# Two operand slices of block 2 spread over block 0's gate steps, the split of blocks 2 and 3's gate operands swapped between VectorE and GpSimd, and the last outputs stored as whole rows

## The chip, the cores and the metric

The kernel runs on one core of a Trainium2 chip. The metric is the time of one execution on the device, in microseconds (us). A profile comes from one further execution, recorded by the hardware; its times are counted from the start of its span.

## What is computed

One layer of a streaming encoder over 2048 prompt tokens and 32 sample tokens, 1024 wide. Cut to the parts that matter here (g_mlp and g_final are weights, p an extra input of 256 columns):

```python
h = x + merge(attention(rmsnorm(x, g_attn) @ w_in)) @ w_out
c = rmsnorm(h, g_mlp)
h = h + square(relu(c @ w_up)) @ w_down
h = h + sigmoid(h @ w_ple_gate) * (p @ w_ple_proj)      # the "gate"
y = rmsnorm(h, g_final)                                 # outputs y_prompt, y_sample
```

All tensors are float32. The keys and values of the attention are outputs too; they are not touched by the change.

## The kernel before, in words

The 2080 tokens are worked in four blocks (0 to 3; 512, 512, 512 and 544 tokens). Activations lie transposed, features on the partitions, in slices of 128 features (index k, 8 slices for 1024).

**Products.** Every float32 operand is split in a high part (ScalarE copies it to the matmul's type, L181) and a low part, raw minus high. The low part is made by GpSimd in pieces of at most 272 columns (`pool_tt`, L166 and L176) or by VectorE in one instruction (L187). Each product is three matmuls (`mm3`): high x high at L216, weight's high x activation's low at L217, weight's low x activation's high at L218. A weight unit is loaded raw into one of four buffers (`wr`) and split in two halves into `piece` tiles from a ring. All DMAs are issued by SyncE (SP), in its order.

**The gate** (`gate`, from L1327) of a block first splits the 8 slices of h into `hu` (block 0 has them made earlier; block 3 puts them in `hc`), then makes 8 steps d: a weight unit of `w_ple_gate`, 24 matmuls into `gps` (8 slices k x 3), the sigmoid of it by ScalarE (L1366 to L1371) and VectorE (L1370), 6 matmuls into `pps`, and VectorE's product (L1385), added to h by GpSimd. Step d's weights are split in two halves of four slices each: the first half serves k = 0 to 3, the second k = 4 to 7.

**What runs beside block 0's gate.** The MLP of block 2 (`mlp7`) works on seven sums and differences of the quarters of its operand c, held split in tiles `cs` for the whole MLP. `cparts` makes them slice by slice, four slices in all, two of which are made earlier. One slice is 2 loads `tmp<-hS` and 2 normalisations on VectorE (L1021), 4 sums (L1033 to L1036, VectorE), and 7 splits of 256 columns: high parts on ScalarE, 5 low parts on VectorE, 2 on GpSimd. The four sums form a chain, since each overwrites a quarter that the next reads. The first step of `mlp7` loads the first two w_up units and makes sums of them (L1259 to L1262, VectorE) and their splits (`lead`). `weave(main, side, 1)` takes one step of the side generator after each step of the main one; with `along` as the side, gate steps 1 and 2 are each followed by a slice of `cparts`, step 3 by nothing, step 4 by the first step of `mlp7` (the gate's step 0 is taken ahead of the weave).

**The order.** The program is written as such generators, and a scheduler then places each engine's instructions with a timeline of its own; so an engine's order is not the written one, and it is shown below where it matters. Each engine then works strictly in that order.

**The end.** `final` (L1393) of block 3 transposes h back, sums the squares, and scales: per 128 tokens the left 512 columns by ScalarE in place (`yn`, L1434), the right 512 by VectorE from the accumulator into `yo` (L1436), each then stored by a DMA of its own, 10 in all.

Of the kernel before, what the change touches and what calls it, by code (L numbers as in the profile page):

```python
# [13 lines left out]
F32 = mybir.dt.float32  # L14
# [6 lines left out]
P = 128  # L21
D = 1024
# [12 lines left out]
BLK = 544  # L35
# [64 lines left out]
def weave(main, side, step, i=0, n=1):  # L100
    for _ in main:
        if i % step == 0:
            for _ in range(n):
                next(side, None)
        i += 1
    drain(side)
# [37 lines left out]
class Kern:  # L144
# [1182 lines left out]
    def gate(self, b, h, up, act, md, wk=None, made=None):  # L1327
        nc, a = self.nc, self.a
        n, t0 = BN[b], 512 * b
# [5 lines left out]
        if made is not None:  # L1335
            hH, hL = made
        elif wk is None and act.aw is None:
            hc = [act.tile([P, 4, 272], F32R, tag="cs", name="hc").rearrange("p a b -> p (a b)") for _ in range(8)]
            hH, hL = [[hc[4 * i + k // 2][:, BLK * (k % 2) : BLK * (k % 2) + n] for k in range(8)] for i in range(2)]
        elif wk is None:  # L1340
            hH = act.tile([P, 8, act.aw], F32R, tag="act", name="hH")
            hL = act.tile([P, 8, act.aw], F32R, tag="act", name="hL")
            hH, hL = [[t[:, k, :n] for k in range(8)] for t in (hH, hL)]
        else:
            hH, hL = [[up.tile([P, BLK], F32R, tag="u", name="hu")[:, :n] for k in range(8)] for _ in range(2)]
        if made is None:
            for k in range(8):
                self.split(hH[k], hL[k], h[:, k, :n], "act", "dve" if k % 2 else "pool")
        for dq in range(2):
            ph, pl = self.wunit(  # L1350
                Wp[:, 512 * dq : 512 * dq + 512].rearrange("(k p) c -> p k c", p=P), [2, 512]
# [38 lines left out]
                        self.pool_tt(hv, hv, sg, ALU.add)  # L1390
                yield

    def final(self, b, h, up, fk, mm, md=None):  # L1393
        nc, a = self.nc, self.a
        t0 = 512 * b
        sts, yns = {}, {}
        phased = md is not None

        def side(c0, tn, q):
            if phased:  # L1400
                sts[c0] = st_all[:, c0 // P]
            elif q == 0:
                sts[c0] = fk.tile([P, 2], F32, tag="fst", bufs=6, name="fst")
            st = sts[c0]
            yp = (md if phased and q == 1 else mm).tile([P, 512], F32, tag="mm", name="yp")
            for k in range(4):
                nc.tensor.transpose(yp[:tn, P * k : P * k + P], h[:, 4 * q + k, c0 : c0 + tn], self.ident)  # L1407
            if phased and q == 1:
                yns[c0, q] = yp
            else:  # L1410
                yns[c0, q] = up.tile([P, BLK], F32, tag="u", name="yn")[:, :512]
                if phased:
                    nc.vector.tensor_tensor(yns[c0, q][:tn], yp[:tn], self.gf[:tn, :512], op=ALU.mult)
                else:
                    nc.vector.tensor_copy(yns[c0, q][:tn], yp[:tn])
            junk = up.tile([P, BLK], F32, tag="u", name="junk")[:tn, :512]
            nc.scalar.activation(junk, yp[:tn], AF.Square, accum_out=st[:tn, q : q + 1])

        if phased:
            st_all = fk.tile([P, 5, 2], F32, tag="fsa", name="fsa")  # L1420
            nc.gpsimd.memset(st_all, 1.0)
            for c0, tn in toks(b):
                side(c0, tn, 0)
                yield
        def emit(c0, tn, r):
            tt = t0 + c0
            dst = a["y_prompt"][0, tt : tt + tn] if tt < SP else a["y_sample"][0, tt - SP : tt - SP + tn]
            for q in range(2):
                src = yn = yns[c0, q]
                if phased and q == 1:  # L1430
                    yn = up.tile([P, BLK], F32, tag="u", name="yo")[:, :512]
                g = self.gf[:tn, 512 * q : 512 * q + 512]
                if phased and q == 0:
                    nc.scalar.activation(yn[:tn], src[:tn], AF.Copy, scale=r)  # L1434
                else:
                    nc.vector.scalar_tensor_tensor(yn[:tn], src[:tn], r, g, op0=ALU.mult, op1=ALU.mult)  # L1436
                self.dma(dst[:, 512 * q : 512 * q + 512], yn[:tn])

        if phased:
            for c0, tn in toks(b):  # L1440
                side(c0, tn, 1)
            ss = fk.tile([P, 5], F32, tag="fss", name="fss")
            nc.vector.tensor_tensor(ss, st_all[:, :, 0], st_all[:, :, 1], op=ALU.add)
            r = self.rsqrt(fk, ss, 5, 1.0 / D, EPS, nc.vector, "rfa")
            for i, (c0, tn) in enumerate(toks(b)):
                emit(c0, tn, r[:tn, i : i + 1])
            return
        for c0, tn in toks(b):
            side(c0, tn, 0)
            side(c0, tn, 1)  # L1450
            st = sts[c0]
            nc.vector.tensor_tensor(st[:tn, 0:1], st[:tn, 0:1], st[:tn, 1:2], op=ALU.add)
            emit(c0, tn, self.rsqrt(fk, st[:tn, 0:1], 1, 1.0 / D, EPS, nc.vector, "rf", tn, 5))
            yield

    def run(self):
        tc, nc, a = self.tc, self.nc, self.a
        with ExitStack() as top:
# [180 lines left out]
            next(g)  # L1639
            box = []  # L1640
            m = self.mlp7(2, hh[1], box, ops[2], wk, up, mm, md)
            weave(g, self.along(c, m), 1)
            f = self.final(0, h, up, fk, mm)
            for _ in range(2):
                next(m)
            h = box[0]
# [12 lines left out]
            h = box[0]  # L1659
            weave(m, f, 1)  # L1660
            g = self.gate(3, h, up, cs, md)
            f = self.final(3, h, up, fk, mm, md)
            for _ in range(5):
                next(g)
            for _ in range(3):
# [46 lines left out]
```

## Time and profile before

| what | value |
|---|---|
| time, median of 3 executions | 3150.33 us (3146.29 to 3152.24) |
| the profiled execution's own time | 3146.42 us |
| its span | 3144.6 us |
| TensorE busy | 3011.4 us, 96% of the span |
| VectorE, ScalarE, GpSimd busy | 60%, 60%, 59% |
| granted TensorE clock, mean | 0.985 |
| block 0's gate | about 2233 to 2286 us |
| block 2's gate | 2641 us on |
| last 10 stores issued | 3136.15 to 3141.41 us |

In a timeline a row gives start, duration, engine (PE is TensorE, DVE VectorE, ACT ScalarE, POOL GpSimd, SP SyncE), line, operation, written and read tiles, and in brackets how long the engine stood idle ahead of it and what released it. A row with xN stands for N such instructions in a run.

### The profile page before, as it was taken

To read this page: it belongs to the slowest core of one execution; us is meant where nothing else is said; L and a number is where in the kernel's file an instruction comes from. 1 tells how busy PE (TensorE), PEld (TensorE's weight loads), DVE (VectorE), ACT (ScalarE), POOL (GpSimd) and SP (SyncE) were. 2 spreads that over 40 slices of the span, in tenths; PEclk is the share of its full clock that TensorE was granted. 3 is DMA by queue.
4 is the path that set the end of the run, shared out by engine and by line. 5 is a ranking of instruction groups with operands and counts; after the bars stand their busy time and mean duration, and the time that the engine had idled before them with its cause. 6 is when DMAs were issued, how large, how long until landed. Compare 5 with 4: busy or idle time off the path is not lost. (4 is left out here: it accounts for less than half of the span.)

```text
span 3144.6 us, 52811 instructions
## 1 busy us (share of the span) xinstructions
PE 3011.4 (96%) x17913; PEld 2649.6 (84%) x17913; DVE 1897.6 (60%) x4596; ACT 1878.1 (60%) x4166; POOL 1847.6 (59%) x2496
## 2 busy tenths in 40 slices
PE   8999898999999999999999999999899999999998
PEld 7787786899977887878788888878788887999998
DVE  5157774645465654666756556535667885576653
ACT  6257775766676764776666656554555455554545
POOL 2357455332345644665655545667877888667674
PEclk9999999999999999999999999999999999999999
DMA  8788757986788746555564543437533446333231
GB/s 281 244 244 244 204 185 229 263 232 201 205 250 230 218 130 153 152 154 153 157 184 130 144 123 103 145 116 241 179 128 115 144 152 229 123 107 107 88 116 56
DMA packets 523287, 539.27 MB, mean 171 GB/s; under 512 B 38749, under 2 KB 401569, under 8 KB 523017
## 3 DMA queue, kind: packets, MB, share of 16 engines
q1 hardware_dynamic: 523016, 535.89, 57.5%
q8 instruction: 142, 2.33, 0.3%
q14 instruction: 129, 1.05, 0.1%
HBM read 421.97 MB, written 117.75 MB: 172 GB/s over the span
## 5 line engine op out<-in xcount | busy, mean ns | idle before, releaser
L176 POOL TENSOR_TENSOR wl<-wr,wh 128x256 fp32r<-128x256 f32 x648 | 475.6, 766 | 354.8 <-ACT wh L181 315.7
L181 ACT ACTIVATE piece<-wr 128x512 fp32r<-128x512 f32 x406 | 246.1, 626 | 272.7 <-PE ups L217 113.1
L176 POOL TENSOR_TENSOR piece<-wr,piece 128x256 fp32r<-128x256 f32 x404 | 327.4, 837 | 99.7 <-ACT piece L181 86.4
L181 ACT ACTIVATE wh<-wr 128x1024 fp32r<-128x1024 f32 x228 | 241.2, 1058 | 171.7 <-PE qps L217 40.7
L166 POOL TENSOR_TENSOR wl<-wr,wh 128x256 fp32r<-128x256 f32 x264 | 199.4, 787 | 194.1 <-ACT wh L181 183.9
L216 PE MATMUL dps<-uh,piece 128*128 128x272 f32 (+1 forms) x768 | 247.0, 325 | 7.5 <-ACT piece L181 3.2
L166 POOL TENSOR_TENSOR piece<-wr,piece 128x256 fp32r<-128x256 f32 x280 | 237.0, 878 | 26.9 <-ACT piece L181 21.5
L218 PE MATMUL dps<-uh,piece 128*128 128x272 f32 (+1 forms) x768 | 247.8, 325 | 1.6 <-POOL piece L166 1.3
L217 PE MATMUL dps<-ul,piece 128*128 128x272 f32 (+1 forms) x768 | 247.8, 323 | 0.0
L216 PE MATMUL ups<-cs,piece 128*128 128x256 f32 (+1 forms) x864 | 246.0, 285 | 1.0 <-DVE r L1232 1.0
L217 PE MATMUL ups<-cs,piece 128*128 128x256 f32 (+1 forms) x864 | 245.3, 284 | 0.0
L218 PE MATMUL ups<-cs,piece 128*128 128x256 f32 (+1 forms) x864 | 245.2, 284 | 0.0
L216 PE MATMUL qps<-aH,wh 128*128 128x512 f32 (+1 forms) x640 | 231.2, 361 | 7.3 <-ACT kn L506 4.0
L218 PE MATMUL qps<-aH,wl 128*128 128x512 f32 (+1 forms) x640 | 229.5, 359 | 0.0
L217 PE MATMUL qps<-aL,wh 128*128 128x512 f32 (+1 forms) x640 | 228.5, 357 | 0.0
L1173 DVE TENSOR_TENSOR h<-h,dps 128x512 f32<-128x512 f32 x256 | 174.3, 683 | 80.9 <-PE dps L218 75.4
L1221 DVE TENSOR_TENSOR h<-h,dps 128x272 f32<-128x272 f32 (+1 forms) x384 | 189.3, 515 | 51.8 <-PE dps L218 50.8
L216 PE MATMUL dps<-uh,wh 128*128 128x512 f32 x512 | 207.8, 406 | 9.4 <-DVE h L1173 5.7
L216 PE MATMUL ups<-cH,wh 128*128 128x512 f32 x512 | 202.8, 396 | 2.1 <-ACT cH L181 1.1
L638 PE MATMUL s<-ka,q 128*128 128x512 f32 (+3 forms) x768 | 187.2, 345 | 15.9 <-ACT e L652 7.1
L218 PE MATMUL dps<-uh,wl 128*128 128x512 f32 x512 | 201.7, 394 | 0.5 <-POOL wl L166 0.4
L217 PE MATMUL ups<-cL,wh 128*128 128x512 f32 x512 | 201.2, 393 | 0.0
(317 smaller groups left out, 9634.2 us busy)
## 6 DMA issues: line engine op xcount, KB each, us to landing
wr<-w_up SPq DMA_DIRECT2D x128, 512.0 KB, 4.0
wr<-w_down SPq DMA_DIRECT2D x128, 512.0 KB, 3.8
wr<-w_in SPq DMA_DIRECT2D x74, 512.0 KB, 5.1
q<-qS SPq DMA_DIRECT2D x128, 256.0 KB, 5.4
v<-vSa SPq DMA_DIRECT2D x64, 512.0 KB, 3.9
ka<-kS SPq DMA_DIRECT2D x32, 512.0 KB, 8.9
wr<-w_out SPq DMA_DIRECT2D x32, 512.0 KB, 4.7
wr<-w_ple_gate SPq DMA_DIRECT2D x32, 512.0 KB, 4.3
```

Of the source, the lines that this page charges most:

```text
L166: nc.gpsimd.tensor_tensor(out[:, sl], a[:, sl], b[:, sl], op=op)
L176: nc.gpsimd.tensor_tensor(out[:, sl], a[:, sl], b[:, sl], op=op)
L181: nc.scalar.activation(hi, raw, AF.Copy)
L216: nc.tensor.matmul(ps, lh, rh, start=start and i == 0, stop=False)
L217: nc.tensor.matmul(ps, lh, rl, start=False, stop=False)
L218: nc.tensor.matmul(ps, ll, rh, start=False, stop=stop and i == n - 1)
L638: nc.tensor.matmul(s, q[:, m, hl, P * qi : P * qi + nr], kt[:, m, k0 - kb : k0 - kb + n], start=hl == 0, stop=hl == 1)
L1173: nc.vector.tensor_tensor(hv, hv, ps, op=ALU.add)
L1221: nc.vector.tensor_tensor(hv, hv, ps, op=ALU.add)
```

## The change

Three edits.

1. In `gate`, for blocks 2 and 3, the low parts of the even slices of h go to VectorE and those of the odd ones to GpSimd; before it was the other way round. Four slices each, as before.
2. Block 0's gate: the two slices of `cparts` follow gate steps 1 and 3 (before: 1 and 2), and the first step of `mlp7` follows step 5 (before: 4).
3. `final` of block 3 takes the pool of the `cs` tiles: both halves of 128 tokens are written into one tile `yo` of 1024 columns, and one DMA stores it: 5 stores in place of 10 (4 of 512 KB, one of 128 KB).

```diff
-                self.split(hH[k], hL[k], h[:, k, :n], "act", "dve" if k % 2 else "pool")
+                self.split(hH[k], hL[k], h[:, k, :n], "act", "dve" if k % 2 == (b < 2) else "pool")
...
+            whole = wide.tile([P, 4, 272], F32, tag="cs", name="yo").rearrange("p a b -> p (a b)") if phased else None
             for q in range(2):
                 src = yn = yns[c0, q]
-                if phased and q == 1:
-                    yn = up.tile([P, BLK], F32, tag="u", name="yo")[:, :512]
+                if phased:
+                    yn = whole[:, 512 * q : 512 * q + 512]
...
-                self.dma(dst[:, 512 * q : 512 * q + 512], yn[:tn])
+                if not phased:
+                    self.dma(dst[:, 512 * q : 512 * q + 512], yn[:tn])
+            if phased:
+                self.dma(dst, whole[:tn, :D])
...
-            weave(g, self.along(c, m), 1)
+            weave(g, chain(islice(c, 1), (None,), c, (None,), islice(m, 1)), 1)
...
-            f = self.final(3, h, up, fk, mm, md)
+            f = self.final(3, h, up, fk, mm, md, cs)
```

The instruction streams differ at four places only: block 0's gate, block 2's gate, block 3's gate, and the last stores.

**Block 0's gate, ScalarE.** `piece_26220` and `piece_26225` are the high parts of the two halves of step 4's gate weights; `cs_...<-tmp_26055` and `tmp_26052` belong to the first of the two slices of block 2's operand, `tmp_26129` to the second; `sig` is the sigmoid of step 2. ScalarE's rows up to the second half, before:

```order
L181 ACTIVATE piece_26299<-wr_26292 128x512
L1366 ACTIVATE sig_26113<-gps_26088 128x512
L1367 ACTIVATE sig_26113<-sig_26113 128x512
L181 ACTIVATE cs_25579<-tmp_26055 128x256
L1368 ACTIVATE sig_26113<-sig_26113 128x512
L181 ACTIVATE cs_25577<-tmp_26052 128x256
L181 ACTIVATE cs_25571<-tmp_26129 128x256
L181 ACTIVATE cs_25575<-tmp_26052 128x256
L181 ACTIVATE piece_26225<-wr_26218 128x512
```

And of the change:

```order
L181 ACTIVATE piece_26278<-wr_26271 128x512
L1366 ACTIVATE sig_26113<-gps_26088 128x512
L181 ACTIVATE lead_26324<-wr_26325 128x512
L181 ACTIVATE cs_25579<-tmp_26055 128x256
L1367 ACTIVATE sig_26113<-sig_26113 128x512
L181 ACTIVATE cs_25577<-tmp_26052 128x256
L1368 ACTIVATE sig_26113<-sig_26113 128x512
L181 ACTIVATE cs_25575<-tmp_26052 128x256
L181 ACTIVATE cs_25583<-tmp_26055 128x256
L181 ACTIVATE piece_26225<-wr_26218 128x512
```

The second slice's split has left the rows ahead of `piece_26225`; the first slice's last one (`cs_25583`, which reads what L1036 writes) has come in, right ahead of it.

**Block 0's gate, VectorE.** The rows up to the sum that ScalarE's last `cs` row ahead of `piece_26225` reads (L1035 before, L1036 of the change). Before, the last 12 of the 15 rows that run without a pause from the landing of the second w_up unit; the three ahead of them are L1260, L1370 and L1021:

```order
L1261 TENSOR_TENSOR wr_26272<-s2_26282,wr_26272 128x4x128
L187 TENSOR_TENSOR lead_26271<-s2_26282,lead_26271 128x512
L1021 SCALAR_TENSOR_TENSOR tmp_26055<-tmp_26055,g_mlp_s_244,r_25489 128x512
L1385 TENSOR_TENSOR sig_26036<-sig_26036,pps_26042 128x512
L1262 TENSOR_TENSOR wr_26274<-wr_26274,s2_26282 128x4x128
L187 TENSOR_TENSOR cs_25574<-tmp_26055,cs_25573 128x256
L187 TENSOR_TENSOR cs_25582<-tmp_26055,cs_25581 128x256
L1033 TENSOR_TENSOR tmp_26055<-tmp_26055,tmp_26052 128x256
L1034 TENSOR_TENSOR tmp_26052<-tmp_26052 128x256
L1021 SCALAR_TENSOR_TENSOR tmp_26129<-tmp_26129,g_mlp_s_244,r_25489 128x512
L187 TENSOR_TENSOR cs_25580<-tmp_26055,cs_25579 128x256
L1035 TENSOR_TENSOR tmp_26052<-tmp_26055,tmp_26052 128x256
```

Of the change, the last 12 rows up to L1036; the four ahead of them are L1259, L1370 and two L1021:

```order
L1385 TENSOR_TENSOR sig_26036<-sig_26036,pps_26042 128x512
L1260 TENSOR_TENSOR s2_26335<-wr_26327,wr_26325 128x512
L187 TENSOR_TENSOR cs_25574<-tmp_26055,cs_25573 128x256
L187 TENSOR_TENSOR cs_25582<-tmp_26055,cs_25581 128x256
L1261 TENSOR_TENSOR wr_26325<-s2_26335,wr_26325 128x4x128
L1033 TENSOR_TENSOR tmp_26055<-tmp_26055,tmp_26052 128x256
L187 TENSOR_TENSOR lead_26324<-s2_26335,lead_26324 128x512
L1034 TENSOR_TENSOR tmp_26052<-tmp_26052 128x256
L187 TENSOR_TENSOR cs_25580<-tmp_26055,cs_25579 128x256
L1035 TENSOR_TENSOR tmp_26052<-tmp_26055,tmp_26052 128x256
L187 TENSOR_TENSOR cs_25578<-tmp_26052,cs_25577 128x256
L1036 TENSOR_TENSOR tmp_26055<-tmp_26055,tmp_26052 128x256
```

L1262 and the second slice's L1021 have moved behind; L1036 and one more low part have come ahead, and L1259 now stands behind the landing that L1260 stood behind before, because SP loads the two w_up units one place later each, with a gate unit ahead of them.

**Block 0's gate, SP.** The loads behind the last two gate units, for the next chunk of `mlp7` (`wr_26585` and `wr_26587` are its two w_up units, 26676 and 26770 w_down units), as a piece of the difference:

```order
 L157 DMA wr_26398<-w_ple_gate 128x8x128
 L157 DMA wr_26585<-w_up 128x4x256
+L157 DMA wr_26676<-w_down 128x2x512
 L157 DMA wr_26587<-w_up 128x4x256
 L157 DMA wr_26770<-w_down 128x2x512
-L157 DMA wr_26676<-w_down 128x2x512
 L157 DMA wr_26858<-w_up 128x4x256
```

A w_down unit has moved ahead of the second w_up unit. The buffers go round in this order, so 26587 has taken the buffer that 26770 had before, that of the last gate unit (26398): it is free only when GpSimd has made the low part `piece_26406` of it.

**Block 2's gate, GpSimd.** `hu_30725` to `hu_30732` are the low parts of the slices k = 0 to 7 of h; 30768, 30773 and 30849, 30854 are the weight halves of the first two gate steps. A piece of the difference:

```order
 L176 TENSOR_TENSOR piece_30773<-wr_30765,piece_30772 128x256 x2
-L166 TENSOR_TENSOR hu_30725<-h_26464,hu_30717 128x256 x2
 L176 TENSOR_TENSOR piece_30849<-wr_30846,piece_30848 128x256 x2
 L176 TENSOR_TENSOR piece_30854<-wr_30846,piece_30853 128x256 x2
-L166 TENSOR_TENSOR hu_30727<-h_26464,hu_30719 128x256 x2
-L166 TENSOR_TENSOR hu_30729<-h_26464,hu_30721 128x256 x2
-L166 TENSOR_TENSOR hu_30731<-h_26464,hu_30723 128x256 x2
+L166 TENSOR_TENSOR hu_30726<-h_26464,hu_30718 128x256 x2
+L166 TENSOR_TENSOR hu_30728<-h_26464,hu_30720 128x256 x2
+L166 TENSOR_TENSOR hu_30730<-h_26464,hu_30722 128x256 x2
+L166 TENSOR_TENSOR hu_30732<-h_26464,hu_30724 128x256 x2
```

Before, GpSimd made slice 0 ahead of the second step's weights and slices 2, 4, 6 behind them; of the change it makes slices 1, 3, 5, 7, all four behind them.

More of the change, by code (lines that the diff above doesn't have):

```diff
@@ L1391, in gate, with final @@
                 yield
-    def final(self, b, h, up, fk, mm, md=None):
+    def final(self, b, h, up, fk, mm, md=None, wide=None):
         nc, a = self.nc, self.a
```

## The prediction, made before the changed kernel was run

> **What bounds the kernel now.** I read the page's busy shares first, then TensorE's waits around the four places where the streams differ, then the timelines of the engines waited for.
>
> ```profile
> span 3144.6 us, 52811 instructions
> PE 3011.4 (96%) x17913; PEld 2649.6 (84%) x17913; DVE 1897.6 (60%) x4596; ACT 1878.1 (60%) x4166; POOL 1847.6 (59%) x2496
> ```
>
> TensorE is the bound and the change leaves all its matmuls in place. So only its 133 us of idle (3144.6 - 3011.4) can change, and of these only what lies at the four places. The waits of TensorE from 2180 to 2320 us, which holds block 0's gate, and from 2600 to 2720, which holds block 2's:
>
> ```profile
> PE gps L216 <- ACT piece L181: 6.5, 1, 6.5
> PE gps L218 <- POOL piece L176: 1.6, 1, 1.6
> PE dps L216 <- ACT uh L181: 1.2, 1, 1.2
> ```
>
> ```profile
> PE gps L217 <- POOL hu L166: 1.9, 2, 1.7
> ```
>
> From 3040 to 3130, block 3's gate, no wait is listed, and TensorE is busy throughout:
>
> ```profile
> 3060.00:3070.00 10.00, 10.00 (x82) 10.00 (x81) 6.90 (x14) 5.00 (x9) 10.00 (x12) 1.00 0.22 70
> ```
>
> (Columns: TensorE, weight loads, VectorE, ScalarE, GpSimd, clock, DMA share, GB/s.) So the whole prize is about 11 us in 3150, and the big wait is the one to understand.
>
> **Block 0's gate, the wait of 6.5 us.** TensorE stops in the middle of gate step 4, for the second half of its weights:
>
> ```profile
> 2250.24 0.50 PE L218 MATMUL gps<-hu,piece 128*128 128x512 f32 x1 [1.60 <-POOL piece L176]
> 2250.58 0.40 PE L216 MATMUL gps<-hu,piece 128*128 128x512 f32 x1
> ...
> 2252.45 0.39 PE L218 MATMUL gps<-hu,piece 128*128 128x512 f32 x1
> 2259.30 0.80 PE L216 MATMUL gps<-hu,piece 128*128 128x512 f32 x1 [6.46 <-ACT piece L181]
> ...
> 2262.87 0.40 PE L218 MATMUL gps<-hu,piece 128*128 128x512 f32 x1
> ```
>
> The nine matmuls from 2259.30 to 2262.87 follow 0.45 apart; the nine from 2250.58 to 2252.45 follow (2252.45 - 2250.58) / 8 = 0.233 apart. So the restart is slow and loses another 8 x 0.21 = 1.7 us. Most that the edit can win here: 1.6 + 6.46 + 1.7 = 9.8 us.
>
> ScalarE makes that half when its queue lets it:
>
> ```profile
> 2258.31 0.42 ACT L181 ACTIVATE cs<-tmp 128x256 fp32r<-128x256 f32 x1 [1.31 <-DVE tmp L1035]
> 2258.63 0.62 ACT L181 ACTIVATE piece<-wr 128x512 fp32r<-128x512 f32 x1
> ```
>
> The raw unit is there (the first half comes from it too); the second half stands behind a `cs` split that waits for VectorE's L1035. VectorE got there by an unbroken run that starts when a w_up unit lands:
>
> ```profile
> 2245.37 0.69 DVE L1260 TENSOR_TENSOR s<-wr 128x512 f32<-128x512 f32 x1 [2.62 <-DMA wr<-w_up]
> ...
> 2247.24 1.23 DVE L1261 TENSOR_TENSOR wr<-s,wr 128x512 f32<-128x512 f32 x1
> ...
> 2249.53 1.21 DVE L1021 SCALAR_TENSOR_TENSOR tmp<-tmp,g_mlp_s,r 128x512 f32<-128x512 f32 x1
> ...
> 2251.26 0.68 DVE L1262 TENSOR_TENSOR wr<-wr,s 128x512 f32<-128x512 f32 x1
> 2251.86 1.82 DVE L187 TENSOR_TENSOR cs<-tmp,cs 128x256 fp32r<-128x256 f32 x2
> ...
> 2254.58 0.83 DVE L1034 TENSOR_TENSOR tmp<-tmp 128x256 f32<-128x256 f32 x1
> ...
> 2257.34 0.94 DVE L1035 TENSOR_TENSOR tmp<-tmp 128x256 f32<-128x256 f32 x1
> ```
>
> 15 instructions from 2245.37 to 2258.28, 12.9 us, with GpSimd busy beside it (fifth of the busy times):
>
> ```profile
> 2250.00:2255.00 5.00, 2.60 (x10) 1.80 (x10) 4.93 (x7) 2.78 (x7) 5.00 (x6) 1.00 0.23 80
> ```
>
> The same L1035 beside an idle GpSimd takes less than half:
>
> ```profile
> 2224.63 0.41 DVE L1035 TENSOR_TENSOR tmp<-tmp 128x256 f32<-128x256 f32 x1
> ```
>
> Now the changed order. The second slice leaves ScalarE's rows ahead of the half, but the last split of the **first** slice (`cs_25583`) comes ahead of it, and that needs L1036, the end of the chain. VectorE's run up to L1036 is 16 instructions: the 15 less L1262 (0.60 from start to start) and one L1021 (1.14), plus L1259 (0.60 to 1.15), one low part of 256 columns (0.33 to 0.87) and L1036 (0.87). It starts at the same landing, 2245.4, because the second of SP's two slots for w_up there now carries the first unit. Summed by the same classes: 12.83 - 1.74 + 1.80 to 2.89 = 12.9 to 14.0, against 12.83 before; then ScalarE's split, as before. So the half starts 0.1 to 1.2 us later. L1260 may be held a little besides, for the second unit takes the place in SP's queue of a gate unit:
>
> ```profile
> 2246.69 0.38 SPq L157 DMA_DIRECT2D wr<-w_ple_gate  x1
> ```
>
> This place opens about 1.4 us sooner, since GpSimd has one `lead` unit fewer ahead of the split that frees the buffer; with 4.3 us to landing (a row below) the unit is there at 2249.6, about when VectorE comes to it; up to 0.5. I take **+0.7 us**. Ends: +1.7 (all slow and the landing late: 1.2 + 0.5), and -4.4, which is the same 16 instructions at the durations beside an idle GpSimd (0.33 to 0.60 from start to start, some 8.5 us). The sum goes by the contended end, since GpSimd's rows in the new order are the same instructions, less one split of a second-slice operand and the lower part of one gate unit.
>
> The 0.8 us by which GpSimd reaches the first half sooner (one `lead` unit fewer ahead of it) shortens the 1.6 wait and lengthens the 6.46 one: nothing.
>
> One rule bears on the end at -4.4. The Trainium skill, SBUF — State Buffer, section "Who interferes with whom", says that a VectorE instruction with two SBUF inputs and a GpSimd instruction that reads SBUF take one shared port pair as an exclusive lock, the later one waiting until the earlier is done. The 0.41 against 0.94 above agrees in kind; by the rule in full each two-input row would cost its own 0.41 and the rest of a GpSimd instruction of about 0.9, so the run would stay at the slow end and the term would be +1.7.
>
> **Behind it.** The next chunk's second w_up unit now takes the buffer that GpSimd frees last, and a w_down unit goes ahead:
>
> ```profile
> 2270.47 0.92 SPq L157 DMA_DIRECT2D wr<-w_up  x2
> 2280.03 0.88 SPq L157 DMA_DIRECT2D wr<-w_down  x2
> 2291.73 0.37 SPq L157 DMA_DIRECT2D wr<-w_up  x1
> ```
>
> (The next two rows: a load's median time from issue to landing, last column; and ScalarE.)
>
> ```profile
> wr<-w_up SPq DMA_DIRECT2D x6, 512.0 KB, 4.3
> ```
>
> ```profile
> 2277.99 1.14 ACT L181 ACTIVATE piece<-wr 128x512 fp32r<-128x512 f32 x2
> ```
>
> Before, both were out by 2271.4 and there by about 2275; the w_down at 2280.03 was the one that waited for the low part of the last gate unit. Of the change the second w_up waits for it. That moment comes somewhat sooner (about 2278.3, because GpSimd's additions no longer wait for a VectorE row behind a landing), so it lands near 2282.5, 7 us later than before. ScalarE's split of it is the second of the two at 2277.99; behind it now queue the sigmoids of steps 6 and 7 and the first eviction of `mlp7`. TensorE uses the unit only in the second product of chunk 1:
>
> ```profile
> 2291.70 0.28 PE L216 MATMUL ups<-cs,piece 128*128 128x256 f32 x1
> ```
>
> which is 2291.70 + 12 x 0.118 = 2293.1. So 9 us of slack cover it, and what remains is a load issue at 2291.73 that comes about 1.2 us later in all and lengthens the `dps` wait of 1.2 above: **+0.5 us** on top (ends 0 and +2.2, the latter if all 1.7 us by which the sigmoids lag is passed on).
>
> **Block 2's gate.** TensorE and GpSimd:
>
> ```profile
> 2642.84 0.40 PE L216 MATMUL gps<-hu,piece 128*128 128x512 f32 x1
> 2644.98 0.50 PE L217 MATMUL gps<-hu,piece 128*128 128x512 f32 x1 [1.74 <-POOL hu L166]
> ```
>
> ```profile
> 2637.48 1.43 POOL L166 TENSOR_TENSOR hu<-h,hu 128x256 fp32r<-128x256 f32 x2
> 2639.30 3.29 POOL L176 TENSOR_TENSOR piece<-wr,piece 128x256 fp32r<-128x256 f32 x4 [0.39 <-ACT piece L181]
> 2642.55 5.60 POOL L166 TENSOR_TENSOR hu<-h,hu 128x256 fp32r<-128x256 f32 x6
> ```
>
> Before, slice 0 fits into a pause at 2637.48 and the wait falls on slice 2, the first that GpSimd makes behind the second step's weights. Of the change all four odd slices stand behind those weights, so the first of them, slice 1, is ready when slice 2 was (2644.98) and TensorE waits one slice earlier: three matmuls, 3 x 0.233 = **+0.7 us**. Below that, GpSimd needs 5.60 / 3 = 1.87 per slice and TensorE 6 x 0.233 = 1.40 for two; once VectorE has made its last slice GpSimd's pairs go at about 1.43, as at 2637.48, so no more is lost. Ends: -1.9 (the pause takes weights, all slices come sooner, the wait goes) and +2.3 (all four at 1.87).
>
> **Block 3's gate**: 0. GpSimd has its odd slices ready from about 2 us ahead of TensorE's use, and TensorE's 10.00 in each window says that nothing shows; if that cover is short, up to +1.
>
> **The last stores.**
>
> ```profile
> 3135.40 3.17 ACT L1434 ACTIVATE yn<-yn,rsy 128x512 f32<-128x512 f32 x5 [0.84 <-DVE rsy L231]
> 3135.48 3.37 DVE L1436 SCALAR_TENSOR_TENSOR yo<-yp,rsy,gf 128x512 f32<-128x512 f32 x5
> 3136.15 0.36 SPq L157 DMA_DIRECT2D y_prompt<-yn  x1
> ...
> 3141.41 0.56 SPq L157 DMA_DIRECT2D y_sample<-yo  x1
> ```
>
> ```profile
> 3138.00:3142.00 4.00, 0.00 (x0) 0.00 (x0) 0.86 (x2) 0.57 (x1) 0.00 (x0) 0.50 1.03 383
> ```
>
> Five issues fewer, but the stretch is bound by the 2.23 MB (544 tokens x 1024 x 4 bytes) at 383 GB/s with a share of 1.03, so 5.8 us of data stay. The first store waits for both halves, 0.1 later. What may go is the tail of the last small issue, 3141.41 to about 3142: **-0.4 us** (ends -1.0, +0.5).
>
> **Sum**: 0.7 + 0.5 + 0.7 + 0 - 0.4 = +1.5 us on the profiled execution's 3146.42, that is 3147.9. That execution lies 3.9 below the median of 3150.33; on the median the forecast is **3151.8**.
>
> **Rivals.**
> - *The stall goes.* With one slice less ahead of it, the half is ready when TensorE asks. Then 6.46 + 1.7 go and 1.6 stays in part: 3150.3 - 8.2 + 0.5 + 0.7 - 0.4 = 3142.9. For it: the second slice has left, and the chain may run faster than its contended pace. Against: the row ahead of the half waits for L1036, one link later than L1035, and even the free pace wins 4.4, not 8.2. Chance 0.17 (with the -4.4 case, 3146.7, as its nearer end).
> - *The late w_up unit is what decides* (slower). If its 7 us pass to TensorE, through the queue behind ScalarE's split and the loads that SP holds behind it, the time is 3151.8 + 6.9 = 3158.7. It decides once that unit's split ends later than 2293.1. Against: it should end near 2283.5. Chance 0.14.
> - *The change does not do what it says*: the scheduler's order keeps the wait, and every other term is hidden: 3150.3. That is next to the forecast and shares its verdict.
>
> **How the numbers follow.** A measurement can tell about 0.2%, 6.3 us, from no change. The forecast and the third rival together have 0.67; the first has 0.17, of which some falls within 0.2%, the second 0.14, and 0.02 stays for the unforeseen. Faster by over 0.2%: 0.16; within: 0.67; slower: 0.17. The terms' own ends add up from -7.7 to +7.7, but not all at once; the spread of the runs is 2 to 4 us. The range reaches to 3143.0, near the first rival, and to 3158.0, near the second.
>
> **What would show it.** Right: TensorE's wait in step 4 still 6 to 8 us, released by ScalarE's `piece`, with ScalarE's row ahead of it waiting for L1036; in block 2 the wait of about 2.4 at slice 1; last store's issue near 3140. Wrong: no `gps <- ACT piece` wait in block 0's gate (first rival), or a `ups` wait for a `piece` near 2293 (second). Most in doubt is VectorE's pace beside GpSimd, on which the largest term hangs.

## The result, and the profile after

The change takes 3156.05 us (median of 22 executions, 3149.1 to 3164.65) against 3151.19 before (22, 3145.22 to 3157.07), measured side by side. The ratio is 1.0019 with a 95% interval of 1.0011 to 1.0026: **3.5 to 8.2 us slower**, about 6. The forecast of 3151.8 was +1.5 of the profiled execution. The medians lie 4.9 us apart. The time lies within the range, but the interval leaves out both no change and +1.5.

The profiled execution of the change took 3153.90 us by itself, 7.5 more than that of before:

```profile
span 3152.1 us, 52800 instructions
PE 3015.9 (96%) x17913; PEld 2652.2 (84%) x17913; DVE 1901.9 (60%) x4596; ACT 1877.8 (60%) x4166; POOL 1843.1 (58%) x2496
```

The eleven instructions fewer are five stores and, net, six that only wait for a semaphore. To find where the 7.5 us lie I matched TensorE's 17913 matmuls by their number and took the start after less the start before. That lag is +0.95 at the last output projection ahead of block 0's gate, +1.47 where step 4 restarts, +7.09 at the end of the MLP's second chunk, +6.92 at block 2's gate, and +7.91 at TensorE's end. So 5.6 of the net 7.5 us arise between the restart of step 4 and the end of the second chunk. One execution against one is a rough measure: ahead of block 0's gate, where the two kernels do the same, the lag wanders between -2.3 and +5.5 before it stands at +0.95. TensorE's waits from 2180 to 2320 us show both places:

```profile
PE gps L216 <- ACT piece L181: 8.4, 2, 8.2
PE css L1100 <- DVE u L1232: 2.0, 1, 2.0
PE dps L216 <- ACT uh L181: 1.3, 1, 1.3
PE ups L216 <- DVE r L1232: 1.3, 1, 1.3
...
PE gps L218 <- POOL piece L176: 0.5, 1, 0.5
```

The stall of step 4 stayed (8.2), the 1.6 of `gps L218` ahead of it fell to 0.5, and two waits are new: TensorE waits for VectorE's L1232, the instruction that empties its accumulators in the MLP. Block 2's gate, 2600 to 2720 us:

```profile
PE gps L217 <- POOL hu L166: 2.4, 1, 2.4
```

**The step-4 stall.** TensorE, ScalarE and VectorE of the change; of VectorE the first and the last (L1036) of the 16 instructions that run without a pause:

```profile
2260.77 0.79 PE L216 MATMUL gps<-hu,piece 128*128 128x512 f32 x1 [8.23 <-ACT piece L181]
```

```profile
2259.78 0.42 ACT L181 ACTIVATE cs<-tmp 128x256 fp32r<-128x256 f32 x1 [1.31 <-DVE tmp L1036]
2260.10 0.61 ACT L181 ACTIVATE piece<-wr 128x512 fp32r<-128x512 f32 x1
```

```profile
2246.22 0.69 DVE L1259 TENSOR_TENSOR wr<-wr 128x512 f32<-128x512 f32 x1 [5.30 <-DMA wr<-w_up]
...
2258.81 0.94 DVE L1036 TENSOR_TENSOR tmp<-tmp 128x256 f32<-128x256 f32 x1
```

ScalarE's half stands behind the split that waits for L1036, as foreseen. From the w_up landing to ScalarE's half it is 13.88 us (2260.10 - 2246.22), before 13.26 (2258.63 - 2245.37). The length of this one wait is no measure by itself, for it trades with the wait for `gps L218` ahead of it: e3 (below), which leaves this stage as it was, has 0.5 and 7.6, before 1.6 and 6.5, in sum 8.1 both. The change's sum is 8.7, so it loses 0.6.

**Behind it.** What the new waits hang on, in SP's and VectorE's order. SP from 2273 us on:

```profile
2273.93 0.37 SPq L157 DMA_DIRECT2D wr<-w_up  x1
2274.40 0.45 SPq L157 DMA_DIRECT2D wr<-w_down  x1
2282.45 0.37 SPq L157 DMA_DIRECT2D wr<-w_up  x1
2297.45 0.37 SPq L157 DMA_DIRECT2D wr<-w_up  x1
```

Before, the two w_up units of the second chunk were issued from 2270.47 on, and the third chunk's first at 2291.73. Counted from the restart of step 4, the last one now comes at 36.7 us (2297.45 - 2260.77), before at 32.4. VectorE:

```profile
2272.67 1.23 DVE L187 TENSOR_TENSOR piece<-wr,piece 128x512 fp32r<-128x512 f32 x1
...
2277.78 0.69 DVE L1259 TENSOR_TENSOR wr<-wr 128x512 f32<-128x512 f32 x1 [2.40 <-DMA wr<-w_up]
2278.39 0.68 DVE L1385 TENSOR_TENSOR sig<-sig,pps 128x512 f32<-128x512 f32 x1
...
2286.36 0.69 DVE L1260 TENSOR_TENSOR s<-wr 128x512 f32<-128x512 f32 x1 [4.52 <-DMA wr<-w_up]
...
2294.55 0.69 DVE L1261 TENSOR_TENSOR wr<-s,wr 128x512 f32<-128x512 f32 x1 [2.72 <-POOL piece L176]
...
2301.23 0.69 DVE L1259 TENSOR_TENSOR wr<-wr 128x512 f32<-128x512 f32 x1 [3.07 <-DMA wr<-w_up]
2301.84 0.41 DVE L1232 TENSOR_TENSOR u<-u,ups 128x256 f32<-128x256 f32 x1
...
2302.77 0.41 DVE L1232 TENSOR_TENSOR r<-u,ups 128x256 f32<-128x256 f32 x1
...
2306.13 0.42 DVE L1232 TENSOR_TENSOR r<-t,ups 128x256 f32<-128x256 f32 x1 [2.24 <-ACT t L1230]
```

GpSimd, ScalarE and TensorE, at the rows that matter:

```profile
2279.15 1.43 POOL L166 TENSOR_TENSOR h<-h,sig 128x256 f32<-128x256 f32 x2 [2.38 <-DVE sig L1385]
2280.54 1.88 POOL L176 TENSOR_TENSOR piece<-wr,piece 128x256 fp32r<-128x256 f32 x2
...
2295.99 1.43 POOL L176 TENSOR_TENSOR piece<-wr,piece 128x256 fp32r<-128x256 f32 x2 [1.47 <-ACT piece L181]
```

```profile
2304.16 1.15 ACT L1236 ACTIVATE r<-r 128x512 f32<-128x512 f32 x2 [5.21 <-POOL r L166]
```

```profile
2303.33 0.36 PE L216 MATMUL ups<-cs,piece 128*128 128x256 f32 x1 [1.29 <-DVE r L1232]
2306.94 0.39 PE L1100 MATMUL css<-sh,ones_r 128*128 128x272 f32 x1 [1.95 <-DVE u L1232]
```

Read from the top, this is a chain of five links. (1) The second slice's VectorE rows now run after step 4's restart, and the low part of a weight unit (L187 at 2272.67) stands behind them; before it began at 2270.12. In the change this row frees the buffer of the second chunk's first w_up unit, whose load goes out when the row ends, at 2273.93. Before, that load had another buffer, which a GpSimd row freed, and went out at 2270.47; the buffer of L187 went to the second unit. (2) L1259 waits for it, 2.40 us; the product L1385 is queued behind L1259, and GpSimd's addition to h waits 2.38 us for L1385. (3) So the low part of the last gate unit ends at 2282.42 (2280.54 + 1.88), and the second w_up unit, which now takes that buffer, is issued at 2282.45 and is there when VectorE's L1260 starts at 2286.36. (4) ScalarE's splits, L1261 and GpSimd's last low part follow, to 2297.42; that frees the buffer for the third chunk's first w_up, issued at 2297.45. (5) VectorE's L1259 waits for this load until 2301.23, and the L1232 rows behind it on the same queue, whose products have ended, wait with it. TensorE has no free accumulators and stops, 1.29 us. The second stop, 1.95 us, takes a longer way: GpSimd's row for `r` waits for the late L1232, ScalarE's L1236 waits 5.21 us for GpSimd, ScalarE's eviction L1230 (`t`) is queued behind L1236, and VectorE's L1232 of 2306.13 waits 2.24 us for that `t`. Behind the stops the matmuls from 2309.22 to 2310.93 follow 0.214 apart ((2310.93 - 2309.22) / 8), where 0.118 is usual:

```profile
2309.22 0.41 PE L217 MATMUL ups<-cs,piece 128*128 128x256 f32 x1
...
2310.93 0.41 PE L216 MATMUL ups<-cs,piece 128*128 128x256 f32 x1
```

The granted clock (seventh figure) is 0.50 there; in the 3.42 us ahead, at full clock, TensorE was busy 0.93 us:

```profile
2305.74:2309.16 3.42, 0.93 (x4) 0.67 (x5) 0.92 (x3) 3.42 (x9) 2.84 (x5) 1.00 0.60 198
2309.20:2312.50 3.30, 3.30 (x17) 3.20 (x16) 1.88 (x3) 2.16 (x7) 3.30 (x4) 0.50 0.35 136
```

From the `ups` matmul at 2309.09 to the `dps` matmul at 2313.45 it is 4.36 us; the same matmuls took 2.82 before (2303.55 to 2306.37). So of the 5.6 us 3.2 are waits, 1.5 are this slow stretch, and the rest are some tenths at each restart. The slow stretch does not follow such stops every time: e5 (below) stops for the same 1.3, 2.0 and 1.3 us in the ten microseconds from 2309 on and keeps the full clock:

```profile
2309.00:2319.00 10.00, 5.48 (x42) 4.84 (x41) 4.97 (x9) 6.29 (x13) 7.50 (x10) 1.00 0.83 305
```

Before has the same rows in the same order on VectorE at the fifth link. Counted from the restart, each came about four us earlier, just in time:

```profile
2292.03 0.41 DVE L1232 TENSOR_TENSOR u<-t,ups 128x256 f32<-128x256 f32 x1
2295.67 0.69 DVE L1259 TENSOR_TENSOR wr<-wr 128x512 f32<-128x512 f32 x1 [3.23 <-DMA wr<-w_up]
2296.28 0.41 DVE L1232 TENSOR_TENSOR u<-u,ups 128x256 f32<-128x256 f32 x1
```

L1259 waits 3.23 us there too, and L1232 stands behind it too: a wait of VectorE that stopped TensorE nowhere when it ended 36.4 us after the restart (2295.67 - 2259.30), and for 3.2 us when it ended at 40.5 (2301.23 - 2260.77).

**The last stores** of the change, the stretch that compares with the 383 GB/s of before:

```profile
3146.00:3150.00 4.00, 0.00 (x0) 0.00 (x0) 0.75 (x2) 0.47 (x1) 0.00 (x0) 0.50 1.02 407
```

From the start of TensorE's last matmul to the end of the span it is 12.46 us (3152.1 - 3139.64), before 12.87 (3144.6 - 3131.73): -0.41.

### The profile page after: what moved, and what is told of

It reads as the page before. It is cut to its first block, busy times and chain, and to the rows that moved or that the text cites. A ratio compares the mean times of both kernels' runs of the same rounds, so it can differ in the third digit from the quotient of the medians.

```text
span 3152.1 us, 52800 instructions
## 1 busy us (share of the span) xinstructions
PE 3015.9 (96%) x17913; PEld 2652.2 (84%) x17913; DVE 1901.9 (60%) x4596; ACT 1877.8 (60%) x4166; POOL 1843.1 (58%) x2496
## 5 line engine op out<-in xcount | busy, mean ns | idle before, releaser
L218 PE MATMUL dps<-uh,piece 128*128 128x272 f32 (+1 forms) x768 | 247.6, 325 | 1.9 <-POOL piece L166 1.7
L218 PE MATMUL ups<-cs,piece 128*128 128x256 f32 (+1 forms) x864 | 245.9, 285 | 0.0
L218 PE MATMUL qps<-aH,wl 128*128 128x512 f32 (+1 forms) x640 | 229.6, 359 | 0.0
L1221 DVE TENSOR_TENSOR h<-h,dps 128x272 f32<-128x272 f32 (+1 forms) x384 | 189.3, 513 | 52.2 <-PE dps L218 51.4
L218 PE MATMUL dps<-uh,wl 128*128 128x512 f32 x512 | 202.3, 395 | 0.4 <-POOL wl L166 0.4
L217 PE MATMUL dps<-ul,wh 128*128 128x512 f32 x512 | 201.8, 394 | 0.0
```

The lines of the kernel that those rows point to most:

```text
L217: nc.tensor.matmul(ps, lh, rl, start=False, stop=False)
L218: nc.tensor.matmul(ps, ll, rh, start=False, stop=stop and i == n - 1)
L1221: nc.vector.tensor_tensor(hv, hv, ps, op=ALU.add)
```

## The experiments

The theory is this: edit 2 costs what is lost, through late w_up loads (the chain above). Its rivals are these: edit 1 or edit 3 takes part in it; or what is lost is only the longer stall of step 4; or it lies in the second slice's contention and not in the loads. Each run is compared with the kernel before on the same chip. Beside the ratio I give the **stage**, TensorE's time from the last output projection ahead of block 0's gate to the last matmul ahead of block 2's gate, in the profiled execution: 424.8 us before, 430.7 of the change. Kernels that do not touch this stage gave 426.3 and 426.7 (e3, e2), so differences under about 2 us say nothing.

### Each edit alone

e1 is before with edit 2 alone:

```diff
-            weave(g, self.along(c, m), 1)
+            weave(g, chain(islice(c, 1), (None,), c, (None,), islice(m, 1)), 1)
```

> Only the second edit (slices after gate steps 1 and 3, the MLP's first step after step 5); split and stores as before. Theory A, from the trace of the change: the whole loss comes from this edit and passes through the next chunk's second w_up unit, which is loaded late, so that SP's following w_up load, VectorE's L1259 behind it and the evictions L1232 behind that are late: expected +5 to +7 us, with TensorE waiting for L1232 near the start of the second chunk (css and ups, 3 us in all) and 8 us for the second half of step 4. Rival B: the loss is shared by the other edits (split of block 2, stores) or is spread over the program: here then only +1 to +3.

Measured: ratio 1.0025 (1.0016 to 1.0034), stage 430.0. TensorE's waits from 2300 to 2400 us, and VectorE of e1 at the fifth link:

```profile
PE css L1100 <- DVE u L1232: 1.9, 1, 1.9
...
PE ups L216 <- DVE r L1232: 0.6, 1, 0.6
```

```profile
2311.18 0.69 DVE L1259 TENSOR_TENSOR wr<-wr 128x512 f32<-128x512 f32 x1 [3.17 <-DMA wr<-w_up]
2311.79 0.41 DVE L1232 TENSOR_TENSOR u<-u,ups 128x256 f32<-128x256 f32 x1
```

Edit 2 alone has the whole loss and both waits; the stall of step 4 is 8.2 as with all three edits.

e2 is before with edit 1 alone:

```diff
-                self.split(hH[k], hL[k], h[:, k, :n], "act", "dve" if k % 2 else "pool")
+                self.split(hH[k], hL[k], h[:, k, :n], "act", "dve" if k % 2 == (b < 2) else "pool")
```

> Only the first edit: the low parts of the even slices of h by VectorE and of the odd ones by GpSimd, for blocks 2 and 3. The prediction's own terms: in block 2's gate the wait falls on slice 1 (L217, about 2.4 us in one wait where there were 1.74 and 0.17), so that TensorE enters the pps product 0.7 us later against the matmuls ahead of the gate (ends -1.9 and +2.3); in block 3's gate no wait; the whole within 0.1%. Rival: the swap lets GpSimd's slices come sooner or later elsewhere, which would show as more than 2 us either way.

Measured: 1.0004 (0.9994 to 1.0014), stage 426.7, no wait for L1232. At block 2's gate TensorE waits once, 2.5 us, where before has 1.9 in two waits:

```profile
PE gps L217 <- POOL hu L166: 2.5, 1, 2.5
```

That is the +0.6 by itself. The forecast for this term is confirmed in the trace; the ratio cannot resolve it.

e3 is before with edit 3 alone:

```diff
+            whole = wide.tile([P, 4, 272], F32, tag="cs", name="yo").rearrange("p a b -> p (a b)") if phased else None
...
-                self.dma(dst[:, 512 * q : 512 * q + 512], yn[:tn])
+                if not phased:
+                    self.dma(dst[:, 512 * q : 512 * q + 512], yn[:tn])
+            if phased:
+                self.dma(dst, whole[:tn, :D])
```

> Only the stores as whole rows. The prediction's own term: -0.4 us (between -1.0 and +0.5) in the stretch from TensorE's last matmul to the end of the span, with about 5.5 us of data at about 380 GB/s either way. Rival: half as many, larger transfers change the data rate, which would show as more than 1 us in that stretch.

Measured: 1.0000 (0.9989 to 1.0011); last matmul to end 12.47 us, -0.40 as in the change. It serves as a control for the stage as well: the third chunk's w_up goes out 32.4 us after the restart (before: 32.4), and no wait for L1232 appears, though the execution as a whole was 8.4 us longer than that of before.

### The two halves of edit 2

Edit 2 moves the second slice one step later and the first step of `mlp7` one step later. e4 does the first alone, e5 the second alone.

```diff
-            weave(g, self.along(c, m), 1)
+            weave(g, chain(islice(c, 1), (None,), c, islice(m, 1)), 1)
```

> Slices after gate steps 1 and 3, but the MLP's first step after step 4 as before. Here the two w_up loads of the first chunk stay ahead of the gate unit, and the next chunk's two w_up loads stay together. Theory A1 (the loss hangs on the place of the MLP's first step, which moves the w_up loads): 0 to +1 us, no wait for L1232 in the second chunk beyond the one of before. Theory A2 (the loss hangs on the second slice's VectorE work, which now runs behind step 4 and holds up the low part that frees a w_up buffer): +3 to +5, with the next chunk's w_up issued 3 us later against TensorE than before. In both the stall in step 4 stays at 6 to 7 us, since the half still stands behind the split that follows L1035.

Measured: 1.0012 (1.0004 to 1.0021), stage 430.6; `css` wait 2.0, `ups` 0.3; the third chunk's w_up goes out 36.6 us after the restart; the step-4 stall is 6.1.

```diff
-            weave(g, self.along(c, m), 1)
+            weave(g, chain(c, (None,), (None,), islice(m, 1)), 1)
```

> Both slices after gate steps 1 and 2 as before, only the MLP's first step one gate step later (after step 5). Theory A1 (place of the MLP's first step): +4 to +6 us, a w_down load ahead of the next chunk's second w_up, and waits for L1232 at the second chunk. Theory A2 (late second slice): 0 to +2.

Measured: 1.0020 (1.0010 to 1.0029), stage 430.1; `css` 2.0, `ups` 1.3; the third chunk's w_up goes out at 37.3; the stall is 6.5. TensorE's waits of e5 from 2180 to 2345 us:

```profile
PE gps L216 <- ACT piece L181: 6.5, 1, 6.5
PE css L1100 <- DVE u L1232: 2.0, 1, 2.0
```

Either half is enough, which neither of the two theories allowed for. With the stall at before's 6.5 and the full loss, e5 rules out the stall as its cause. In e4 the load order of before is kept, and by its rows the delay arises from VectorE instead: the second slice's rows push a sigmoid's L1370, for which ScalarE then waits up to 2.9 us, and with it the low parts. So no one changed load is needed; what both have in common is a row that frees a buffer late, and the third chunk's load that goes out 4 to 5 us late for it.

### Is it the third w_up load, and the queue behind it?

Three kernels touch that load. d1 is before with it made twice, one after the other, which was meant to make it late and nothing else:

```diff
-                self.dma(
+                for _ in range(2 if (b, ch, i) == (2, 2, 0) else 1):
+                    self.dma(
```

> The kernel before, with one load done twice: the first w_up unit of block 2's third chunk (the third w_up pair of the MLP), so that it is there about 4 us later. Theory A (the loss of the change is the lateness of this load: VectorE's L1259 waits for it with the evictions L1232 queued behind, and TensorE runs out of free accumulators): TensorE waits for L1232 there (css and ups), 3 us or more in all, although nothing of block 0's gate is changed. Rival C (the load has slack, and the waits in the changed kernel come from the slower sigmoid and splitting rows): no wait for L1232 there, shift below 1 us.

One execution: 3158.80 us, among before's 3149.12 to 3164.39 on that chip; stage 426.6. The expected waits are absent, and VectorE shows why:

```profile
2304.92 0.42 DVE L1232 TENSOR_TENSOR u<-u,ups 128x256 f32<-128x256 f32 x1 [0.23 <-PE ups L218]
...
2315.01 0.69 DVE L1260 TENSOR_TENSOR wr<-wr 128x512 f32<-128x512 f32 x1 [2.58 <-DMA wr<-w_up]
```

The scheduler saw two loads and put the sum (L1260 in this kernel) seven rows later, behind the evictions. The load is there 44.1 us after the restart, later than the change's 40.5, and costs TensorE nothing measurable. So here a late load alone did not stop TensorE; in the change it did, with evictions queued behind the row that waits for it. Since the order moved, this is no clean test of the lateness.

g2 is the change with the same load twice:

> The changed kernel, with the third chunk's first w_up unit loaded twice. By the order of the rows this puts VectorE's L1259 seven rows later, behind the evictions L1232 of the second chunk (and some of TensorE's down products ahead of up products), while gate, split and stores are those of the change. Theory A (the price is a load's wait that stands ahead of the evictions in VectorE's queue): although the load comes still later, no css wait for L1232, and from block 0's gate to block 2's gate TensorE comes out 3 to 5 us ahead of the changed kernel, about +1 to +2 against before. Theory B (the price is the lateness itself, wherever L1259 stands): TensorE waits as long or longer, +5 us or more.

Measured: 1.0013 (1.0000 to 1.0027), stage 430.0. TensorE's waits of g2 from 2300 to 2400 us, in which both waits for L1232 are gone:

```profile
PE dps L216 <- DVE h L1221: 2.1, 1, 2.1
```

Counted by the MLP's `ups` matmuls, g2 is 4.9 us ahead of the change at the end of the third chunk and 1.5 behind it at the end of the fourth. I had expected 3 to 5 back; by block 2's gate it is 0.7. With the queue out of the way in both, g2 still needs 3.4 us more than d1 in the stage (430.0 against 426.6), and its load is there 3.8 later (47.9 us after the restart against 44.1). But this is not the lateness passed on as waits. Both have a wait of 2.0 to 2.1 us for L1221 in the fourth chunk, but behind it g2 runs at half clock, and once more at 2584, which d1 does nowhere in block 2's MLP:

```profile
2369.23:2372.64 3.41, 3.41 (x14) 3.03 (x13) 3.41 (x8) 1.26 (x2) 2.33 (x3) 0.50 0.56 193
```

d2 is the change with that load left out (the sums take the second chunk's unit still in the buffer, so block 2's part of the output is another):

```diff
+                if (b, ch, i) == (2, 2, 0):
+                    raws.append(kept[0])
+                    continue
...
+                if (b, ch, i) == (2, 1, 0):
+                    kept.append(raws[0])
```

> The changed kernel with this same load left out: the third chunk's first w_up unit is taken from the second chunk's used buffer, so the outputs of block 2 differ. Theory A: L1259 has no load to wait for, the css and ups waits for L1232 at the start of the second chunk go (below 0.5 us), and the stage comes back by 3 to 5 us against the changed kernel. Rival C: the waits stay at 2 us and more.

Measured: 1.0009 (0.9999 to 1.0019), stage 428.8. The `css` wait is gone and `ups` is 0.7, so 1.9 of the stage's 5.9 us came back. Here too the following loads moved: the third chunk's second unit went out 45.6 us after the restart, in the change 42.2. That is a direction, not a full account; 3 to 5 had been expected.

How much is waits and how much is clock, over the whole of block 2's MLP (from its first matmul to block 2's gate, profiled executions; TensorE has the same matmuls in all):

| run | length, us | idle | busy |
|---|---|---|---|
| before | 355.2 | 9.1 | 346.1 |
| e2, e3, d1 | 355.7 to 356.6 | 9.5 to 10.4 | 346.1 |
| the change | 360.4 | 12.3 | 348.1 |
| e1, e4, e5 | 359.6 to 359.8 | 10.8 to 12.5 | 347.3 to 348.9 |
| g2 | 359.7 | 11.0 | 348.7 |

The busy time grows because the same matmuls take longer: the kernels of the lower three rows each have 3.4 to 6.8 us at a granted clock of 0.50 in this stretch, the others none. So of the 3.0 to 5.2 us that edit 2, or a half of it, loses here, 1.2 to 2.8 are slower matmuls and the rest are waits; g2 differs from d1 by 2.6 of busy time and 0.8 of idle.

### Can the stall be removed, and does that help?

Three or all four slices made earlier, in the output projection:

```diff
-                weave(g, islice(c, 2), 1)
+                weave(g, islice(c, 3), 1)
...
-            weave(g, self.along(c, m), 1)
+            weave(g, chain(c, (None,), (None,), islice(m, 1)), 1)
```

> From the kernel before: one more slice of block 2's operand is made earlier, in block 3's output projection (three there, one after block 0's gate step 1; the MLP's first step after step 4). Theory: VectorE's run of 13 us in step 4 shrinks by the rows of a slice, so the second half of step 4's weights is no longer late by 6.5 us; if the wait there falls under 2 us, -4 to -7 us. Rival: the splits left ahead of the half still wait for the one slice's chain (L1035 or L1036), and the wait stays over 5 us; then between -1 and +3.

Measured: 1.0015 (1.0004 to 1.0026), stage 430.4; as its rival said, the stall stays, 7.3, and `gps <- DVE hd L980` is 4.0, which was 1.5 before and 1.1 to 2.6 in the kernels that leave this part alone.

f3 has `islice(c, 4)` and `chain((None,), (None,), (None,), islice(m, 1))` in these places:

> As the kernel before, but all four slices are made in block 3's output projection and none in block 0's gate (MLP's first step after step 4). Theory: no split of the operand stands ahead of step 4's half and the stall of 6.5 us goes, with its slow restart: -6 to -9 us in block 0's gate. Rival: the two slices make a wait of their own in the output projection (for VectorE's rows or for the hS loads), which gives back 3 us or more.

Measured: 1.0016 (1.0005 to 1.0027), stage 429.8. TensorE's waits of f3 from 2180 to 2345 us:

```profile
PE gps L216 <- DVE hd L980: 4.2, 2, 2.8
PE gps L216 <- DVE sig L1370: 2.8, 1, 2.8
PE gps L216 <- ACT piece L181: 2.6, 1, 2.6
PE css L1100 <- DVE u L1232: 1.3, 1, 1.3
```

The stall falls to 2.6, and what it gives is spent ahead of it, where VectorE is now late with `hd` (4.2) and with a sigmoid (2.8).

h3 goes the other way, both slices behind steps 3 and 4 and `mlp7` behind step 6:

```diff
-            weave(g, self.along(c, m), 1)
+            weave(g, chain((None,), (None,), c, (None,), islice(m, 1)), 1)
```

> From the kernel before: block 2's two slices behind gate steps 3 and 4, the MLP's first step behind step 6. ScalarE's rows then have both halves of steps 4, 5 and 6 ahead of every operand split. Theory: the stall of 6.5 us in step 4 goes with its slow restart, and as the queue at the second chunk still has L1259 ahead of L1232 with a load that comes later, 3 to 5 us come back there: -4 to 0 in all. Rival: the two slices, now later, hold up the last gate step or the MLP's first products (waits for cs splits), 5 us or more, so that nothing is won: 0 to +6.

Measured: 0.9992 (0.9979 to 1.0004), stage 429.1. Waits from 2180 to 2345 us:

```profile
PE ups L216 <- DVE r L1232: 2.5, 1, 2.5
...
PE css L1100 <- DVE u L1232: 1.9, 1, 1.9
PE gps L216 <- ACT piece L181: 1.9, 1, 1.9
```

At step 4 TensorE is 6.2 us ahead of before; by the end of the second chunk it is 5.5 behind, through L1232 above all. Its profiled execution thus has a longer stage than before (429.1 against 424.8), which its median does not bear out. The same with the third chunk's load made twice:

> The same with the third chunk's first w_up unit loaded twice, which puts L1259 behind the evictions. Theory: the step-4 stall is gone and no wait for L1232 comes in its place: -4 to -8 us. Rival: the load, later still, or the late slices are waited for elsewhere (ups for cs or piece): 0 to +6.

Measured: 0.9996 (0.9984 to 1.0008), stage 426.7: stall 0.2, no `css` wait, and the time comes back in several waits of 0.7 to 2.4 us on VectorE, ScalarE and GpSimd. Neither differs measurably from before, and the second does not reach the -4 us expected of it; both ratios lie below that of the change. No version tried is shown to beat before.

## Why the prediction was right or wrong

**What bounds the kernel** was right as to the place: three quarters of the loss lie at one of the four. "Only its 133 us of idle" was too narrow: of the span's 7.5 us only 3.0 are idle (136.2 against 133.2) and 4.5 are busy, since a matmul at a lower clock counts as longer work; the slow stretch above is in them. That the time fell inside the range is owed to the range's width: the term that carries the loss was put at an eighth of its size. (The lower ends of the terms add up to -7.3, not -7.7.)

**The stall, +0.7: right in size and mechanism.** The 16 instructions took 13.45 us from start to start (the row behind L1036 starts at 2259.67), within the 12.9 to 14.0 forecast at the contended pace, and the half came 0.62 later counted from the landing. With the 1.6 us wait shortened to 0.48 and the 6.46 lengthened to 8.23, both waits together grew by 0.6, and the lag at the restart by 0.5 (1.47 - 0.95). The end at -4.4 did not occur. By the Trainium skill's rule in full (SBUF — State Buffer, "Who interferes with whom") this term would have been +1.7 by the prediction's estimate; the trace gives 0.62, about a third of it, since the pace was no worse than that of the rows quoted from before.

**"Behind it", +0.5: the step that failed, and the mis-sized term.** It measured about +4: 5.6 from the restart to the end of the second chunk, less 1.4 that before waits for L1221 behind it and the change does not. The table of block 2's MLP says the same: 360.4 us against 355.2 to 356.6. Three things in it were wrong. The low part of the last gate unit was put at 2278.3, because GpSimd's additions "no longer wait for a VectorE row behind a landing"; they did wait, 2.38 us, for L1385 behind L1259, because the first w_up load was late too, and the row ended at 2282.4. Then the load issue said to come "about 1.2 us later in all" came 4.3 later (36.7 against 32.4 from the restart). And the slack was measured at the wrong consumer: "9 us of slack cover it" counts to TensorE's own use of the unit at 2293.1, and there it held (the split ended at 2287.0). It was larger still, for the row at 2291.70 is the fifth product of the first chunk; that chunk's seven products are 84 matmuls from 2286.06 on, so the second chunk reads the unit about 4 us later than 2293.1. What ran out was the slack of the **next** load in that buffer, on which VectorE waits with evictions queued behind it. The `dps` wait, which was to lengthen, is 1.3 against 1.2. The slow stretch behind the new waits was in no term.

**The slower rival** ("the late w_up unit is what decides") named the path, ScalarE's split and the loads that SP holds behind it, but its price of +6.9 on the forecast was too high for what came, about 4.5 (about 6 less the forecast's 1.5). Its condition was wrong: it decided though the split ended 6 us ahead of 2293.1. Its sign did not come either: there is no `ups` wait for a `piece` near 2293, but waits for L1232 at 2303 and 2307. A chance of 0.14 was too low, for a condition that watches one consumer only.

**Block 2's gate, +0.7: right in place and mechanism**, one wait in place of two, 2.4 against 1.9 (e2: 2.5), so +0.5 to +0.6. In the lag of the matmuls it does not show whole (+7.09 at the second chunk, +6.92 at the gate, 7.11 behind it). **Block 3's gate, 0: right**; no wait is listed. **The stores, -0.4: right in size**, -0.41 and -0.40 in e3. The reason was right in part only: the data did not stay at 383 GB/s, they went at 407.

**What stays open.** That edit 2 carries the loss, that either half does, and that the stall does not, is shown. That late buffers and loads pass it on is read from the chain in the trace and supported by d2, but every run that took the L1232 waits away also moved other loads or TensorE's order. So how much of the 4 us is owed to VectorE's queue and how much to the lateness of all the loads is not settled, nor why some stops are followed by half clock and others, as in e5 and d1, are not. Another 0.75 us near 2814 us, at a `dps` wait that e1 and e5 have too and e3 and e4 do not, was not followed.

## What to carry to other kernels

When work is moved behind a stage, follow each buffer it frees later through to the next load in that buffer, and to the instruction that waits for that load; and then ask what stands behind that instruction in its engine's queue. Slack counted to the first consumer is not the slack of the chain. Where several engines share a stretch, removing the largest stall may only move it: h3 was 6.2 us ahead at step 4 and had lost more than that within two chunks.

## What the runs showed of the hardware

- **A queue waits as one.** VectorE idled 3.07 us ahead of L1259 for a load while L1232, behind it and ready, stood between TensorE and its accumulators; with L1232 ahead (d1) a load there 3.6 us later still gave no wait for L1232.
- **Short stops can halve TensorE's clock, but need not.** It was not only the stall of 8 us that was followed by slow matmuls (0.45 apart in place of 0.233, in both kernels): after stops of 1.3, 2.0 and 1.3 us within 6 us the granted clock was 0.50 from 2309.2 to 2312.5, the matmuls went 0.214 apart in place of 0.118, and that added 1.5 us to 3.2 of waits. In e5 the same stops left the clock at 1.00. The Trainium skill, TensorE: Matmul & The Clock Gate, "Part 1: The HAM clock gate", gives a clock that is either full or half, and half after an idle window of about 3.4 us. The trace agrees with the halving (0.50); that it takes a whole idle window it does not, for no stop here was longer than 1.95 us, and TensorE was busy 0.93 of the 3.42 us ahead.
- **Whole rows store a little faster**: the same 2.23 MB at 407 GB/s against 383, and 0.4 us less from the last matmul to the end.
